# Four paired slabs in a row in gate and up, with a fifth weight place and the residual outside

## The chip, the cores and the metric

The kernel runs on one core of one Trainium2 chip. The metric is the device time in microseconds (us) of one execution; the time of the kernel before is the median of three runs.

## The reference, cut to what matters

One encoder layer over 256 rows of width 2048, everything in float32: four mixers side by side (gated linear attention, a Fourier mixer, a long convolution, a short convolution) whose outputs are joined and projected, a cross attention to 256 memory rows, a gated feed-forward part with a hidden width of 5632, and a last norm. The change lies in the feed-forward part:

```python
def swiglu(h, w_gate_up, w_down):
    gate, up = jnp.split(h @ w_gate_up, 2, axis=-1)
    return (jax.nn.silu(gate) * up) @ w_down
...
        x = x + mix @ w_out[l]
        x = x + cross_attention(rms_norm(x, norm_g[l, 1]), mem_n, w_xq[l], w_xkv[l], w_xo[l])
        x = x + swiglu(rms_norm(x, norm_g[l, 2]), w_gate_up[l], w_down[l])
    return rms_norm(x, final_norm_g)
```

## The kernel before

**Precision.** TensorE multiplies in a shortened 32-bit form, so each operand is split into a high part (a cast on ScalarE) and a low part (the rest, a subtraction on VectorE). One product of a 128x128 piece of features with a 128x512 piece of weights is three matmuls: high x high, high x low, low x high (`part`, L430 to L435).

**The weight stream.** All weights come as slabs of 128x2048 (1 MB) in the order in which they are used; class `Stream` loads each into one of three raw buffers (SP's queue), casts and subtracts it half by half into a *weight place*, and hands the halves to TensorE. There are three places in the pool `wp`, and a fourth in another pool while `extra` is set; `_fill` (L166) prepares up to three halves beyond the one in use. A half takes its place when TensorE is done with the one that had it.

**Plain and paired slabs.** In gate and up and in down the two row halves of the features and two column blocks of the weights form a 2x2 block product. A *plain* slab (N) holds 16 blocks and needs eight products. A *paired* slab (S) holds two feature blocks for two column blocks each, and does them with seven products (a Winograd scheme): the weights are also added up to sums, which makes four halves of 1024, 512, 1024 and 1024 columns (`_sums`, L140) instead of two of 1024, and the features are added up once into tiles `z` (`combine`, L437). In gate and up the first sum comes from memory ready made: in `_load` the last 512 columns are copied twice into a tile `two` and 1024 columns are accumulated onto it by a DMA from POOL's queue (L99 to L103), so VectorE adds twice per paired slab (L158); in down it adds four times.

**The stages around the change.** Gate and up takes its first 512 + 512 columns with eight plain slabs (L1125), then ten groups of eight slabs each (L1133), with the plan `GROUP`: paired slabs are the third, fifth and seventh. `mixed` (four 512-wide operations on VectorE) follows the last paired slab of a group, `gated` (two) the point at which the gate columns are done as well, `upped` (two additions, two scalings, two transposes, then two stores from POOL's queue to the memory tensor `hidden`) the end of the group. Down then runs over 44 blocks of 128 hidden features in two passes of 22 slabs; `PASSES[0]` begins with four plain slabs. Its first six pairs take slots 0 to 11, so its first plain slab uses slots 12, 13, 14 and 15 (`steps`, L471).

**What sets the order.** Instructions are put on their engines in written order where they can run, and a scheduler moves them up where their data and buffers allow. `keep_place` (L308) ties an instruction to the one written before it on its engine. Small work is written between the products by generators in class `Background` (L204). It keeps a debt of VectorE: `dve(n, ops)` adds n / 960 + 0.155 per operation, each product takes off 0.68 (`pe`, L226), and `poll`, called behind each product, steps a generator only where its time has come and the debt is under `OWED`, 0.9:

```python
    def poll(self):
        for e in list(self.q):
            if self.owed < OWED and self.now >= e[1]:
                self.step(e)
```

One generator is `fetch` (L1087): for block k it loads the turned tile of `hidden` into one of eleven `tmp` buffers (POOL's queue) and, some blocks later and not before 15 us behind the store, splits it into slot k of `f` (a cast on ScalarE and a 256-wide subtraction on VectorE, both tied by `keep_place`). `early` brings slots 0 to 21 while gate and up still runs; behind the last group `drain(early)` (L1135) writes whatever is left of it at once, and a second `fetch` brings the rest, which `ready` (L1188) forces block by block, three ahead of use.

**Memory.** `res` is the residual, four tiles of 128x1024 that gate and up does not touch. Slots of `f` are `act[4:12]`, fourteen tiles of their own, the three `z` tiles in halves, and the normed features `h3`.

Of the kernel before, what the change touches and what calls it, by code (L numbers as in the profile page):

```python
# [13 lines left out]
F32 = mybir.dt.float32  # L14
# [9 lines left out]
P = 128  # L24
# [20 lines left out]
GROUP = "NNSNSNSN"  # L45
# [3 lines left out]

PAIRED = {a + i for a, plan in [(GATE_UP + 8 * j, GROUP) for j in range(10)] + [(DOWN, PASSES[0]), (DOWN + 22, PASSES[1])]  # L50
          for i, x in enumerate(plan) if x == "S"}
SUMMED = {i for i in PAIRED if i < DOWN}

# [18 lines left out]
class Stream:  # L72


    def __init__(self, tc, pools, W, bg):
# [8 lines left out]
        self.extra = self.sums = None  # L84
# [3 lines left out]
    def _buffers(self, n, m):  # L88

        pool = self.extra if self.extra and len(self.halves) % 4 == 3 else self.wp  # L90
        at = 48 if any(a <= n < b for a, b in ROWS) else 8
        return (pool.tile([P, 1088], F32R, name=t, tag=t)[:, at:at + m] for t in ("wh", "wl"))

    def _load(self, n):
# [3 lines left out]
        if n // 16 + 1 in SUMMED:  # L98
            W, t = self.W[n // 16 + 1], self.sums.tile([P, 1024], F32, name="two", tag="two")  # L99
# [66 lines left out]
    def _fill(self):  # L166

        ahead = self.at + 1 + min(3 if self.extra else 2, self.n // 16)
        while len(self.halves) < ahead and self.made < NBLK:
            self._half()  # L170

# [82 lines left out]
class Block:  # L254
# [208 lines left out]
    def paired_rows(self, w, cols, slots, sums, plan, mixed, first, ready=None, late=0, before=None, swap=False):  # L463
# [12 lines left out]
        def put(name, hi, lo, wh, wl):  # L476
# [5 lines left out]
            left[name] -= 1  # L482
            self.part(q[name][:, :], hi, lo, wh, wl, new, left[name] == 0)

        form = lambda t, r: (t[:, r * P:(r + 1) * P], t[:, R + r * P:R + (r + 1) * P])
        n = done = 0
        for i, kind in enumerate(plan):
            if before:
                before(i)
            if kind == "S":  # L490
# [76 lines left out]
    def run(self):  # L567
# [21 lines left out]
        self.gk = [nc.dram_tensor(f"state{i}", (R, P), F32, kind="Internal").ap() for i in range(4)]  # L589
        self.vd = nc.dram_tensor("values", (P, 8 * 512), F32, kind="Internal").ap()  # L590
# [18 lines left out]
        with self.tc.tile_pool(name="wx", bufs=1) as st.extra:  # L609
# [257 lines left out]
    def attention(self, ps):  # L867
        tc, nc, act, st = self.tc, self.nc, self.act, self.st
        with tc.tile_pool(name="atp", bufs=1) as atp, tc.tile_pool(name="kp", bufs=1) as kp, \
# [111 lines left out]
            st.extra = None  # L981
# [47 lines left out]
    def mlp(self):  # L1029
        tc, nc, act = self.tc, self.nc, self.act  # L1030
        with tc.tile_pool(name="fp", bufs=1) as fp:
            self.gap(fp, 192)
            f = [fp.tile([P, 512], F32R, name=f"f{i}") for i in range(14)]
            z = [fp.tile([P, 1024], F32R, name=f"z{i}") for i in range(3)]
            f = act[4:12] + f + [z[i // 2][:, i % 2 * 512:i % 2 * 512 + 512] for i in range(6)] + self.h3
            with tc.tile_pool(name="wy", bufs=1) as self.st.extra:
                self.gap(self.st.extra, 64)
                with tc.tile_pool(name="tw", bufs=2) as self.st.sums, tc.tile_pool(name="gp", bufs=1) as gp:
# [8 lines left out]
    def gate_up(self, gp, f, z):  # L1047
# [74 lines left out]

        sums = [((2 * i, 2 * i + 1), z[i]) for i in range(GROUP.count("S"))]
        comb = self.bg.add(combined())
# [766 lines left out]
```

## Time and profile before

| what | us |
|---|---|
| median of 3 runs (lowest, highest) | 1436.53 (1435.76, 1437.61) |
| the profiled execution's own time | 1434.72 |
| its span | 1432.9 |
| TensorE busy | 1423.0 (99%) |
| VectorE busy | 1145.7 (80%) |
| ScalarE busy | 815.8 (57%) |

The span is the stretch that the profile covers; the profiled execution's own time is 1.82 us longer, and the median of the runs 1.81 us longer than that. Engines in the profile: PE is TensorE's matmuls, PEld its weight loads, DVE VectorE, ACT ScalarE, POOL GpSimd, SP the engine whose queue issues most loads. A timeline row has start, length, engine, source line, operation, out<-in and count, and in brackets the idle time before it with what ended it. Matmuls overlap, so their spacing counts, not their length.

### The profile page before, as it was taken

The page shows a single profiled execution, that of the slowest core. Times are in us where ns is not written, and L with a number is a line of the kernel's source. Part 1 is how long each engine was busy: PE and PEld are TensorE (multiplying, and loading weights), DVE is VectorE, ACT ScalarE, POOL GpSimd, SP SyncE. Part 2 cuts the span into 40 slices and gives each one's busy share as a digit, 9 for nine tenths or more (in the row PEclk, how much of TensorE's full clock was granted, in tenths as well). Part 3 has the DMA queues.
Part 4 walks back from the last instruction along what each step waited for, and adds up shares of the span by engine and source line. Part 5 has one row for each costly group of instructions (what it writes and reads, how often), then busy time and mean ns, then how long its engine had stood idle before and what let it go on. Part 6 is the DMA issues. An engine that isn't in the chain of part 4 may idle for free.

```text
span 1432.9 us, 18653 instructions
## 1 busy us (share of the span) xinstructions
PE 1423.0 (99%) x6589; PEld 1181.4 (82%) x6589; DVE 1145.7 (80%) x1738; ACT 815.8 (57%) x1183; POOL 234.6 (16%) x306
## 2 busy tenths in 40 slices
PE   9999999999999999999999999999999999999997
PEld 8888888888888888888888888888888888788886
DVE  6667868777877767777677888889888888989997
ACT  7556565446745555556455556555555556655655
POOL 0000100013212223531430121122011002000000
PEclk9999999999999999999999999999999999999999
DMA  9877554456667787865986989899999887665554
GB/s 350 299 291 247 205 202 166 171 172 224 198 199 232 235 271 246 275 201 171 287 242 207 283 280 289 275 275 285 294 293 289 264 265 227 217 231 180 193 219 147
DMA packets 73038, 343.80 MB, mean 240 GB/s; under 512 B 10957, under 2 KB 12654, under 8 KB 45168
## 3 DMA queue, kind: packets, MB, share of 16 engines
q1 hardware_dynamic: 54848, 288.98, 57.6%
q0 software_dynamic: 17664, 52.97, 15.6%
q8 instruction: 51, 0.84, 0.2%
q10 hardware_dynamic: 432, 0.66, 0.1%
q14 instruction: 43, 0.35, 0.1%
HBM read 322.12 MB, written 20.45 MB: 239 GB/s over the span
## 4 chain that ended last, share of the span: by engine, by line
PE 98%; DVE 1%; DMA 0%; ACT 0%; issue 0%; SPq 0%; ACTq 0%
PE pg L432 22%; PE pg L433 22%; PE pg L434 22%; PE pm L432 7%; PE pm L434 7%; PE pm L433 7%; PE pg L380 4%; PE pg L381 2%; PE pm L1344 1%; PE pm L1022 1%; PE pm L993 1%; PE pm L1753 0%; DMA raw<-in_W 0%; DVE res L282 0%; PE pm L994 0%; PE pm L1518 0%
## 5 line engine op out<-in xcount | busy, mean ns | idle before, releaser
L136 DVE TENSOR_TENSOR wl<-raw,wh 128x1024 fp32r<-128x1024 f32 (+1 forms) x413 | 494.1, 1211 | 167.6 <-ACT wh L135 164.8
L135 ACT CAST wh<-raw 128x1024 fp32r<-128x1024 f32 (+1 forms) x413 | 424.7, 1043 | 282.9 <-PE pg L434 188.3
L432 PE MATMUL pg<-wh,act 128*128 128x512 f32 (+1 forms) x1191 | 465.5, 391 | 0.0
L433 PE MATMUL pg<-wl,act 128*128 128x512 f32 (+1 forms) x1191 | 463.9, 389 | 0.1
L434 PE MATMUL pg<-wh,act 128*128 128x512 f32 (+1 forms) x1191 | 463.8, 390 | 0.0
L432 PEld LDWEIGHTS pg<-wh,act 128*128 128x128 f32 x1191 | 224.0, 188 | 47.9 <-issue 1.5
L434 PEld LDWEIGHTS pg<-wh,act 128*128 128x128 f32 x1191 | 223.9, 188 | 47.5 <-DVE act L282 0.6
L433 PEld LDWEIGHTS pg<-wl,act 128*128 128x128 f32 x1191 | 224.0, 188 | 46.5 <-DVE wl L136 1.2
L147 ACT CAST wh<-raw 128x1024 fp32r<-128x1024 f32 (+1 forms) x150 | 137.4, 921 | 149.6 <-PE pg L434 53.8
L148 DVE TENSOR_TENSOR wl<-raw,wh 128x1024 fp32r<-128x1024 f32 (+1 forms) x150 | 155.9, 1060 | 52.8 <-ACT wh L147 52.6
L433 PE MATMUL pm<-wl,act 128*128 128x512 f32 x309 | 120.3, 389 | 0.1
L432 PE MATMUL pm<-wh,act 128*128 128x512 f32 x309 | 120.2, 389 | 0.0
L434 PE MATMUL pm<-wh,act 128*128 128x512 f32 x309 | 120.2, 389 | 0.0
L380 PE MATMUL pg<-act,wh 128*128 128x512 f32 x256 | 90.5, 395 | 0.0
L381 PE MATMUL pg<-act,wl 128*128 128x256 f32 x256 | 71.8, 280 | 0.0
L433 PEld LDWEIGHTS pm<-wl,act 128*128 128x128 f32 x309 | 58.0, 188 | 12.3 <-DVE wl L136 0.4
L434 PEld LDWEIGHTS pm<-wh,act 128*128 128x128 f32 x309 | 58.0, 188 | 12.1
L432 PEld LDWEIGHTS pm<-wh,act 128*128 128x128 f32 x309 | 58.0, 188 | 12.0
L102 POOL DMA_DIRECT2D two<-in_W x30 | 26.6, 885 | 237.6 <-DMA two<-in_W 106.4
L158 DVE TENSOR_TENSOR raw<-raw 128x512 f32<-128x512 f32 x90 | 61.8, 687 | 1.2
L147 ACT CAST wh<-two 128x1024 fp32r<-128x1024 f32 x30 | 31.5, 1051 | 52.0 <-PE pg L434 27.0
L380 PEld LDWEIGHTS pg<-act,wh 128*128 128x128 f32 x256 | 48.1, 188 | 10.5
(375 smaller groups left out, 1819.3 us busy)
## 6 DMA issues: line engine op xcount, KB each, us to landing
raw<-in_W SPq DMA_DIRECT2D x216, 1024.0 KB, 5.6
raw<-in_W SPq DMA_DIRECT2D x30, 768.0 KB, 6.3
two<-in_W SPq DMA_DIRECT2D x60, 256.0 KB, 4.8
two<-in_W POOLq DMA_DIRECT2D x30, 512.0 KB, 9.0
raw<-in_W SPq DMA_DIRECT2D x11, 512.0 KB, 7.1
hidden<-g POOLq DMA_DIRECT2D x22, 256.0 KB, 3.8
tmp<-hidden POOLq DMA_DIRECT2D x44, 128.0 KB, 6.0
features<-tmp POOLq DMA_DIRECT2D x32, 128.0 KB, 5.2
```

Of the source, the lines that this page charges most:

```text
L102: nc.gpsimd.dma_start(t, W[:, 512:1536], accum_op=ALU.add)
L135: nc.scalar.copy(wh[:, a:b], r[:, a:b])
L136: nc.vector.tensor_tensor(out=wl[:, a:b], in0=r[:, a:b], in1=wh[:, a:b].bitcast(F32), op=ALU.subtract)
L147: nc.scalar.copy(wh, src)
L148: nc.vector.tensor_tensor(out=wl, in0=src, in1=wh.bitcast(F32), op=ALU.subtract)
L158: nc.vector.tensor_tensor(out=out, in0=a, in1=b, op=ALU.add)
L380: self.nc.tensor.matmul(p[:, :], wh, slot[:, :], start=start, stop=False)
L381: self.nc.tensor.matmul(p[:, 0:R], wl, slot[:, 0:R], start=False, stop=stop)
L432: self.nc.tensor.matmul(p, hi, wh, start=start, stop=False)
L433: self.nc.tensor.matmul(p, hi, wl, start=False, stop=False)
L434: self.nc.tensor.matmul(p, lo, wh, start=False, stop=stop)
L993: nc.tensor.matmul(p[:, :], q[d][:, r * P:(r + 1) * P], kt[d][:, :], start=d == 0, stop=False)
```

## The change

The plan of a group becomes two plain slabs, four paired in a row, two plain (`GROUPS`). The residual is stored to memory during gate and up's first slabs, its four tiles take the ready made sums in turn (`st.sums`), and it is loaded back behind the tenth group. `AHEAD` says with which earlier slab each ready made sum is loaded (slab 2 of a group with slab 6 of the group before, 3 with 0, 4 with 1, 5 with 3). The two `two` tiles go, and a fifth weight place `wz` comes in their room; places now form a list `ring`, the one used longest ago first, to which pools are lent and given back. There are four `z` tiles and twelve own `f` tiles, so `early` brings slots 0 to 19 and the second `fetch` 20 to 43. In gate and up each product is tied by `keep_place`. The code also knows a kind "s" (paired, without a ready made sum), which the plan does not use.

```diff
-GROUP = "NNSNSNSN"
+GROUPS = "NNSSSSNN",
...
+AHEAD = {2: -2, 3: 0, 4: 1, 5: 3},
+SUMS = {GATE_UP + 8 * j + a: GATE_UP + 8 * j + i for j in range(10) for i, a in AHEAD[j % len(GROUPS)].items()}
...
     def _buffers(self, n, m):
-        pool = self.extra if self.extra and len(self.halves) % 4 == 3 else self.wp
+        slot = min(self.ring, key=lambda x: x[1])
+        assert slot[1] < self.at or slot[1] < 0
+        pool, slot[1] = slot[0], len(self.halves)
...
-        if n // 16 + 1 in SUMMED:
-            W, t = self.W[n // 16 + 1], self.sums.tile([P, 1024], F32, name="two", tag="two")
+        if n // 16 in SUMS:
+            W, t = self.W[SUMS[n // 16]], self.sums[0]
+            self.sums.append(self.sums.pop(0))
...
-        ahead = self.at + 1 + min(3 if self.extra else 2, self.n // 16)
+        ahead = self.at + 1 + min(len(self.ring) - 1, self.n // 16)
...
+            mark = self.mark()
             self.part(q[name][:, :], hi, lo, wh, wl, new, left[name] == 0)
+            if w == "w_gate_up":
+                self.keep_place(mark)
...
-            f = [fp.tile([P, 512], F32R, name=f"f{i}") for i in range(14)]
-            z = [fp.tile([P, 1024], F32R, name=f"z{i}") for i in range(3)]
+            f = [fp.tile([P, 512], F32R, name=f"f{i}") for i in range(12)]
+            z = [fp.tile([P, 1024], F32R, name=f"z{i}") for i in range(4)]
...
-        sums = [((2 * i, 2 * i + 1), z[i]) for i in range(GROUP.count("S"))]
+        sums = [((2 * i, 2 * i + 1), z[(i + 1) % 4]) for i in range(4)]
...
+        def before(n):
+            if n == 1:
+                self.st.lend(self.wz)
+                for c, x in enumerate(whole):
+                    nc.sync.dma_start(self.rd[:, c * 1024:(c + 1) * 1024], x)
+                self.st.sums = list(whole)
+            if n in (1, 3):
+                self.bg.drain(self.late if n == 1 else last)
...
-        early = self.bg.add(fetch(0, FT - 22, 3, 2.0, 15))
+        early = self.bg.add(fetch(0, FT - 24, 3, 2.0, 15))
         self.bg.drain(comb)
         for j in range(1, DFF // 512):
-            upped(j, self.paired_rows("w_gate_up", [j * 512, DFF + j * 512], self.h3, sums, GROUP, mixed, gated, swap=j % 2 == 0)[0])
+            plan = GROUPS[(j - 1) % len(GROUPS)]
+            upped(j, self.paired_rows("w_gate_up", [j * 512, DFF + j * 512], self.h3, sums[:8 - plan.count("N")], plan, mixed, gated,
+                                      before=lambda i: (j, i) == (10, 5) and self.st.back(self.wz), swap=j % 2 == 0)[0])
+        for c, x in enumerate(whole):
+            nc.sync.dma_start(x, self.rd[:, c * 1024:(c + 1) * 1024])
         self.bg.drain(early)
-        self.fetch = self.bg.add(fetch(FT - 22, FT, 6, SOON))
+        self.fetch = self.bg.add(fetch(FT - 24, FT, 6, SOON))
```

More of the change, by code (lines that the diff above doesn't have):

```diff
@@ L83, in __init__ @@
         self.raw = None
-        self.extra = self.sums = None
+        self.ring = [[self.wp, -1] for _ in range(3)]
+        self.sums = []
         self.places = []
@@ L166, in _fill, with lend, back @@
     def _fill(self):
-        ahead = self.at + 1 + min(3 if self.extra else 2, self.n // 16)
+        ahead = self.at + 1 + min(len(self.ring) - 1, self.n // 16)
         while len(self.halves) < ahead and self.made < NBLK:
             self._half()
+    def lend(self, pool):
+        self.ring.append([pool, -1])
+        return pool
+    def back(self, pool):
+        self.ring = [x for x in self.ring if x[0] is not pool]
     def _used(self):
@@ L608, in run @@
         nc.scalar.copy(self.identr, self.ident)
[L609 removed]
+        with self.tc.tile_pool(name="wx", bufs=1) as self.wx:
+            st.lend(self.wx)
             self.attention(self.mixers())
```

25 lines of the change are left out of this document (14 added, 11 removed).

## The prediction

> **What bounds the kernel now.** I read the page first (engine shares, chain), then the windows table cut at the ten groups, then timelines of one group and of the passage from gate and up to down.
>
> ```profile
> PE 1423.0 (99%) x6589; PEld 1181.4 (82%) x6589; DVE 1145.7 (80%) x1738; ACT 815.8 (57%) x1183; POOL 234.6 (16%) x306
> ...
> PE 98%; DVE 1%; DMA 0%; ACT 0%; issue 0%; SPq 0%; ACTq 0%
> ```
>
> The chain is TensorE for 98% of the span, so a matmul taken away shortens the kernel unless another wait fills its place. The windows table: gate and up's first slabs, two of the ten groups, the passage, the first part of down:
>
> ```profile
> core 0: us, PE busy (x) PEld busy (x) DVE busy (x) ACT busy (x) POOL busy (x), PEclk, DMA share, GB/s
> 690.00:775.00 85.00, 85.00 (x377) 70.24 (x375) 61.11 (x108) 48.16 (x73) 26.11 (x33) 1.00 0.82 254
> ...
> 982.00:1023.50 41.50, 41.50 (x185) 34.37 (x184) 36.88 (x47) 24.49 (x30) 7.06 (x9) 1.00 0.92 275
> ...
> 1106.50:1148.00 41.50, 41.50 (x185) 34.38 (x184) 35.20 (x41) 23.26 (x25) 3.83 (x5) 1.00 0.90 268
> ...
> 1189.50:1231.00 41.50, 41.47 (x184) 34.01 (x183) 38.93 (x62) 24.18 (x39) 12.98 (x15) 1.00 0.82 254
> 1231.00:1317.00 86.00, 85.96 (x378) 70.38 (x377) 79.47 (x133) 50.49 (x74) 0.00 (x0) 1.00 0.53 196
> ```
>
> TensorE has no gap in a group, VectorE is busy 85 to 89% of it, and the DMA engines 90 to 92%. So the gain is certain to be asked for, and two engines stand close behind. One product (three matmuls) takes 0.68 us, from the starts of two successive L432 in TensorE's timeline:
>
> ```profile
> 982.00 0.39 PE L432 MATMUL pg<-wh,act 128*128 128x512 f32 x1
> ...
> 982.68 0.39 PE L432 MATMUL pg<-wh,act 128*128 128x512 f32 x1
> ```
>
> **Term 1, the fourth paired slab.** A plain slab is eight products, a paired one seven. A group goes from 5 x 8 + 3 x 7 = 61 products (41.5 us, as the row) to 60 (40.8). Ten groups: 10 x 0.68 = 6.8 us less on the path.
>
> **Term 2, four paired slabs in a row against VectorE.** VectorE's timeline over one paired slab:
>
> ```profile
> 1001.33 1.82 DVE L148 TENSOR_TENSOR wl<-raw,wh 128x1024 fp32r<-128x1024 f32 x2
> 1003.07 0.68 DVE L158 TENSOR_TENSOR raw<-two,raw 128x512 f32<-128x512 f32 x1
> 1003.78 0.69 DVE L158 TENSOR_TENSOR raw<-raw 128x512 f32<-128x512 f32 x1
> 1004.39 0.41 DVE L282 TENSOR_TENSOR f<-tmp,f 128x256 fp32r<-128x256 f32 x1
> 1005.05 1.23 DVE L148 TENSOR_TENSOR wl<-two,wh 128x1024 fp32r<-128x1024 f32 x1 [0.24 <-ACT wh L147]
> ...
> 1019.45 3.50 DVE L136 TENSOR_TENSOR wl<-raw,wh 128x1024 fp32r<-128x1024 f32 x3 [0.21 <-ACT wh L135]
> ```
>
> Three subtractions in 3.50 us with a last one of 1.22 start 1.14 apart. The first two of the slab take 1.74 to the next start (1.14 + 0.60), the two additions 0.71 + 0.61. A paired slab is 3 x 1.14 + 0.60 + 1.32 = 5.34 us of VectorE against 7 x 0.68 = 4.76 of TensorE; a plain one 2.28 against 5.44. Per group VectorE grows by 5.34 - 2.28 = 3.1 us, to about 38.3 of 40.8: it fits on average, but inside the run it falls behind by 0.58 us a slab. What covers it is the fifth place, four halves ready while one is in use. The refill, from ScalarE's timeline beside TensorE's:
>
> ```profile
> 987.90 0.39 PE L434 MATMUL pm<-wh,act 128*128 128x512 f32 x1
> ...
> 988.37 1.05 ACT L147 CAST wh<-raw 128x1024 fp32r<-128x1024 f32 x1 [0.29 <-PE pm L434]
> ```
>
> The last matmul of a half would be followed at 988.13, the cast starts 0.25 later and takes 1.05, the subtraction follows. Let the run start at 0: its first four halves are ready, half 5 is split by 0.25 + 1.05 + 1.2 = 2.5, and VectorE then works without rest: 4.4 after half 6 and its additions, 6.7 after half 8, then 5.34 a slab. The tightest half is the third of the last slab, ready at 6.7 + 5.34 + 1.14 + 0.60 + 1.32 + 1.14 = 16.2; TensorE asks for it at 3 x 4.76 + 3 x 0.68 = 16.3. It holds by 0.1 us. With four places it would not (each refill starts a half later). Every 0.1 us more per slab costs 0.3 a group, 3 us in all. Bounds: 0 and 6 us (0.2 a slab off). I take 0.5, near the end the rows give.
>
> **Term 3, the planner's debt and what it holds back.** This is the term that decides. The background generator `fetch` brings the gated products back and splits them into the slots that down needs; it steps only where the planner's debt is under 0.9. The debt is counted from the code: a 1024-wide half 1.22, a 512-wide operation 0.69, two 512 additions 1.38, a 256-wide split 0.42; each product takes off 0.68. Before, a group adds 10 x 1.22 + 3 x 5.73 for the halves and 8.26 for `mixed`, `gated` and `upped`: 37.7 against 61 x 0.68 = 41.5, so it returns to nothing in each group and four splits a group go through. By that count the 22nd is written in the sixth group's slab 5. The trace agrees (these are the casts of the 22 splits):
>
> ```profile
> L290 ACT CAST act<-tmp x8: 397/401/404, 794.3 to 880.5; 128x256 fp32r<-128x256 f32 x8
> ...
> L290 ACT CAST f<-tmp x14: 398/400/402, 885.6 to 1013.6; 128x256 fp32r<-128x256 f32 x14
> ```
>
> After, a group adds 8 x 1.22 + 4 x 5.73 + 8.26 = 40.95 against 60 x 0.68 = 40.80. The debt never runs off: each group ends 0.15 higher, 0.42 more for each split. Counted half by half (halves written four ahead) its lowest points, at the end of a group's second slab, are 0 in the first group (loads only, the split must wait 15 us), 0.29 in the second (one split), 0.87 in the third (one split), then 1.44 and 0.15 more each time, to 2.4 in the tenth. So two of the 20 early splits go through, and 18 wait for `drain(early)` behind the tenth group. `keep_place` ties each to the VectorE instruction written before it, the last transpose of `upped`, so none can be pulled forward. Down's first plain slab starts with slots 12, 13, 14, 15. Before, all were there long before down's first product:
>
> ```profile
> L432 PE MATMUL pg<-wh,f x46: 389/389/393, 1192.8 to 1297.2; 128*128 128x512 f32 x46
> ...
> 1194.64 1.27 DVE L282 TENSOR_TENSOR h<-h,pm 128x512 f32<-128x512 f32 x2
> 1195.84 1.40 DVE L286 SCALAR_TENSOR_TENSOR h<-h,rc,g 128x512 f32<-128x512 f32 x2
> 1197.16 1.29 DVE L557 STREAM_TRANSPOSE g<-h 128x512 f32<-128x512 f32 x2
> 1198.38 3.45 DVE L136 TENSOR_TENSOR wl<-raw,wh 128x1024 fp32r<-128x1024 f32 x3
> ...
> 1203.43 0.76 DVE L282 TENSOR_TENSOR z<-tmp,z 128x256 fp32r<-128x256 f32 x2
> ...
> 1222.13 0.75 DVE L282 TENSOR_TENSOR act<-tmp,act 128x256 fp32r<-128x256 f32 x2
> ```
>
> `upped` takes 1198.38 - 1194.64 = 3.7 us on VectorE after the group's last product; splits follow one another by 0.75 - 0.41 = 0.34. The loads are not tied, and POOL's timeline shows loads of down's late slots issued over 100 us before their splits (the first of those stands at 1203.43 above), as far as the eleven `tmp` buffers go:
>
> ```profile
> 1038.81 3.53 POOL L564 DMA_DIRECT2D tmp<-hidden  x4 [4.59 <-issue]
> ...
> 1081.49 2.65 POOL L564 DMA_DIRECT2D tmp<-hidden  x3 [5.58 <-issue]
> ...
> 1198.15 1.52 POOL L559 DMA_DIRECT2D hidden<-g  x2 [30.44 <-DVE g L557]
> 1205.09 6.18 POOL L564 DMA_DIRECT2D tmp<-hidden  x7 [5.41 <-DVE tmp L282]
> ...
> tmp<-hidden POOLq DMA_DIRECT2D x44, 128.0 KB, 6.0
> ```
>
> So loads 2 to 12 are in their buffers, eleven of them, and load 13 waits for the first split. From the last product at 0: `upped` ends at 3.8, splits 2 to 12 at 3.8 + 11 x 0.34 = 7.5, product of slot 12 from 7.6 (1.36 us of work). POOL stores the hidden tiles first (to about 5.2), load 13 then takes 6.0 and its cast and subtraction 0.8: 12.0. Slots 14 on follow 0.88 apart (6.18 / 7), faster than the 1.36 that TensorE needs. Idle: 7.6, and 12.0 - 7.6 - 1.36 = 3.0: 10.6 us. If load 13 had a buffer too it is 8; if only nine of the eleven are held by these loads, 13. I take 10. What no longer stands there, `mixed` and `gated`, is done two slabs earlier, so VectorE isn't fuller behind the stall; I put nothing for it, at most 3 us for a first paired slab of down whose sums come late.
>
> **Term 4, the clock after the stall.** At the very start TensorE's 256-wide matmuls stand 0.21 us apart, then 0.12:
>
> ```profile
> 1.07 4.64 PE L601 MATMUL pm<-ones 128*128 128x128 f32 x20 [1.07 <-DVE eps L602]
> ...
> 5.72 0.41 PE L433 MATMUL pg<-wl,act 128*128 128x256 f32 x1
> 5.93 0.41 PE L434 MATMUL pg<-wh,act 128*128 128x256 f32 x1
> ...
> 7.11 0.28 PE L434 MATMUL pg<-wh,act 128*128 128x256 f32 x1
> 7.23 0.28 PE L432 MATMUL pg<-wh,act 128*128 128x256 f32 x1
> ```
>
> Half speed lasted up to 6.8, 5.7 us from the first matmul. Before has no idle stretch that shows whether a stall brings it back. If it does, the loss is at most half of 5.7, 2.9 us; if not, nothing. Part of it would lie under the wait for load 13. I take 1. The Trainium skill, "TensorE: Matmul & The Clock Gate", Part 1, says that an idle window of about 3.4 us halves the clock and that some 3.4 us of work release it. By that rule the loss would be about 1.7 us, and it speaks against the change; the starting rows fit it, and no run here yet shows a stall of that length.
>
> **The edits at nothing.** The residual's store (2 MB, four SP issues in gate and up's first slabs) and its return lie in stages with room, 0.82 and 0.53 of the DMA engines by the windows rows, and three raw buffers stand between SP and TensorE. Uncovered, each would be 2.1 MB at the 275 GB/s of the row, 7.6 us. On SP the return stands ahead of raw loads two slabs before use. The fourth `combine` is beside plain slabs. The written order costs nothing: the rows shown run in it already.
>
> **The DMA engines.** One group (the window from 934.87 to 976.36) has these shares by queue (packets, MB, share); the last line is the page's rate by slice:
>
> ```profile
> q1 hardware_dynamic: 2018, 9.18, 63.7%
> q0 software_dynamic: 801, 2.69, 29.7%
> ...
> GB/s 350 299 291 247 205 202 166 171 172 224 198 199 232 235 271 246 275 201 171 287 242 207 283 280 289 275 275 285 294 293 289 264 265 227 217 231 180 193 219 147
> ```
>
> 9.18 MB in 63.7% of 41.5 is 347 GB/s; q0 takes 12.3 us for 2.69 MB. A paired for a plain slab adds 0.26 MB to q1 (0.75 us) and one 0.52 MB accumulation to q0 (2.4 us at q0's rate): 38.8 + 3.2 = 42 us against 40.8, less the loads that no longer pass. The excess is 1.2 us a group at the end where rates stay, nothing where a fuller queue is faster. Loads run two slabs (10 us) ahead, so I put 0.
>
> **Sum.** -6.8 + 0.5 + 10 + 1 = +4.7 us. On the profiled execution, 1434.72 (span 1432.9), that is 1439.4; the median of the runs, 1436.53, is 1.8 above it, so I give 1441.2 for the median.
>
> **The rivals.** A, the splits do pass: something (a debt lower than my count by 0.6 where it is lowest) lets four a group through. Then term 3 and 4 go. For it: eight lowest points are under 2.4, not far from 0.9. Against it: the same count places the 22 splits of before. Price: -6.8, plus a split or two inside the paired run, which has 0.1 us to spare (0.7 us in five groups): -6.8 + 3.5 to -6.8, about 1431.5. B, VectorE loses the run: its order there isn't the written one, or an addition waits; from 0.3 us a slab on, each group loses 0.9, 9 us in ten: -6.8 + 9 + 11 = +13 with term 3, +2 without. For it: a margin of 0.1 us. Against it: before, VectorE idles 4.6 to 6.3 us of each group (the rows above), part of it for lack of a place, and a fifth is added. C, the DMA engines bound the groups: 1.2 us each, +12 on top of -6.8, about +5 without term 3 and +16 with it. For it the 42 against 40.8, against it that fuller queues ran faster: 350 GB/s in the page's first slice. D, the change does less than it says: a product order that already holds can't change time; it decides nothing.
>
> **How the numbers follow.** Term 3 as counted: 0.62. A: 0.23. B: 0.10. C: 0.05. No change is what lies within 0.2% (2.9 us), about what a measurement of this kernel can tell. The likeliest case runs from +1 (8 of stall, no clock loss) to +10, so a quarter of it, 0.16, falls within 0.2%, and 0.02 below for what I may have missed; 0.44 is slower, with B and C 0.59. A gives 0.22 faster and 0.01 the same: 0.24, 0.17, 0.59 in all. Alone the likeliest case has 1437.5 to 1446.5; with A below and B above the range is 1430.5 to 1447.
>
> **What would show it.** Right: group period 40.8 us; TensorE idle some 10 us in one or two pieces behind the tenth group, released by a split on VectorE; the casts of `fetch` absent between the third group and the end; one burst of eighteen. Wrong: casts of `fetch` spread over the groups and no gap there (A); gaps at the fourth paired slab's third half in every group (B); casts waiting for raw with TensorE behind them (C).

## The result and the profile after

The changed kernel takes 1494.6 us (median of 4 runs, 1491.7 to 1496.6) against 1436.1 (median of 4, 1435.4 to 1437.6): a ratio of 1.040, interval 1.0385 to 1.0424. The forecast was 1441.2 with a range up to 1447. Slower was the likeliest side, but the loss, 58.5 us, is twelve times the 4.7 forecast. The profiled execution took 1496.58 us, its span is 1494.5 (before: 1432.9), so 61.6 us have to be found.

Shares and chain of the changed kernel, from its page:

```profile
PE 1440.3 (96%) x6559; PEld 1176.8 (79%) x6559; DVE 1177.0 (79%) x1786; ACT 826.7 (55%) x1205; POOL 243.0 (16%) x316
...
PE 26%; DVE 10%; DMA 7%; issue 7%; ACT 3%; POOL 0%; SPq 0%; ACTq 0%; DVEq 0%; POOLq 0%
```

TensorE is no longer the whole chain (98% before); VectorE and the DMA engines have come into it. The windows table, cut at the same three stages in both kernels, first after, then before:

```profile
690.00:780.00 90.00, 85.41 (x367) 69.78 (x366) 62.08 (x116) 47.89 (x74) 29.26 (x36) 0.96 0.93 291
780.00:1235.00 455.00, 426.47 (x1802) 336.74 (x1801) 377.96 (x438) 238.63 (x271) 57.81 (x68) 0.99 0.87 264
1235.00:1320.00 85.00, 73.81 (x312) 58.60 (x311) 73.94 (x135) 49.09 (x89) 29.58 (x34) 0.96 0.82 227
```

```profile
690.00:780.00 90.00, 90.00 (x399) 74.38 (x398) 64.61 (x113) 50.26 (x75) 26.15 (x34) 1.00 0.81 251
780.00:1195.00 415.00, 415.00 (x1832) 343.71 (x1831) 357.02 (x420) 235.08 (x272) 67.76 (x79) 1.00 0.90 278
1195.00:1280.00 85.00, 84.93 (x373) 69.17 (x372) 79.95 (x141) 50.89 (x82) 12.98 (x15) 1.00 0.63 212
```

Second number is TensorE's busy time. Before it fills all three stages; after it has holes in all three. I added up every start-to-start distance of TensorE's matmuls beyond 0.227 us (its steady distance): 7.3 us are lost in gate and up's first stage, 47.0 in the ten groups, 14.7 in the passage and down's first part. With the 6.8 that the fourth paired slab saves, that is +62.2 against the 61.6 measured (the kernel before loses 1.1 in the same three). The period of a group (distance of the casts of the product q1, first to last of the ten) is 45.8 us; before it was 41.5, and 40.8 was forecast.

The three places, in rows. **The passage**, TensorE's timeline, with ScalarE's casts for down's slots and POOL's loads for them:

```profile
1240.40 0.39 PE L449 MATMUL pm<-wh,act 128*128 128x512 f32 x1
1249.84 0.79 PE L447 MATMUL pg<-wh,f 128*128 128x512 f32 x1 [9.05 <-ACT f L305]
1250.43 0.63 PE L448 MATMUL pg<-wl,f 128*128 128x512 f32 x1
1250.86 0.63 PE L449 MATMUL pg<-wh,f 128*128 128x512 f32 x1
...
1252.57 0.50 PE L447 MATMUL pg<-wh,f 128*128 128x512 f32 x1
1252.91 0.40 PE L448 MATMUL pg<-wl,f 128*128 128x512 f32 x1
1253.14 0.39 PE L449 MATMUL pg<-wh,f 128*128 128x512 f32 x1
```

```profile
1241.25 1.32 ACT L305 CAST f<-tmp 128x256 fp32r<-128x256 f32 x4
...
1249.39 0.40 ACT L305 CAST f<-tmp 128x256 fp32r<-128x256 f32 x1 [5.87 <-DMA tmp<-hidden]
...
1245.38 11.52 POOL L582 DMA_DIRECT2D tmp<-hidden  x13
```

One stall, ended by a split of down's slot (line 305, `fetch`), then matmuls 0.43 apart until 1252.6. The split itself waited for its load, the first of the thirteen that POOL issues from 1245.38 on. **The first stage**, ScalarE's timeline beside TensorE's:

```profile
736.88 2.94 ACT L143 CAST wh<-raw 128x1024 fp32r<-128x1024 f32 x3 [8.97 <-DMA raw<-in_W]
```

```profile
734.60 0.39 PE L449 MATMUL pg<-wh,act 128*128 128x512 f32 x1
738.92 0.80 PE L447 MATMUL pg<-wh,act 128*128 128x512 f32 x1 [3.94 <-ACT wh L143]
740.37 0.80 PE L448 MATMUL pg<-wl,act 128*128 128x512 f32 x1 [0.65 <-DVE wl L144]
740.97 0.63 PE L449 MATMUL pg<-wh,act 128*128 128x512 f32 x1
```

ScalarE waited 9.0 us for a raw load; TensorE stood still for 3.9 us, and for 0.65 more until the subtraction behind the cast was done. **The groups**, the table of waits over nine of the ten groups (total, times, longest), and VectorE's and TensorE's timelines inside one run of four:

```profile
ACT wh L143 <- DMA raw<-in_W: 81.1, 25, 7.3
ACT wh L155 <- DVE raw L166: 54.9, 19, 5.7
...
PE pg L448 <- DVE wl L156: 10.9, 15, 1.5
PE pm L448 <- DVE wl L156: 10.3, 14, 1.5
```

```profile
942.02 0.69 DVE L166 TENSOR_TENSOR raw<-res,raw 128x512 f32<-128x512 f32 x1
942.62 1.22 DVE L156 TENSOR_TENSOR wl<-res,wh 128x1024 fp32r<-128x1024 f32 x1
943.76 0.68 DVE L166 TENSOR_TENSOR raw<-raw 128x512 f32<-128x512 f32 x1
945.01 1.23 DVE L156 TENSOR_TENSOR wl<-res,wh 128x1024 fp32r<-128x1024 f32 x1 [0.57 <-ACT wh L155]
946.16 1.22 DVE L156 TENSOR_TENSOR wl<-raw,wh 128x1024 fp32r<-128x1024 f32 x1
```

```profile
944.92 0.39 PE L449 MATMUL pg<-wh,z 128*128 128x512 f32 x1
945.97 0.49 PE L447 MATMUL pg<-wh,z 128*128 128x512 f32 x1 [0.67 <-ACT wh L155]
947.43 0.50 PE L448 MATMUL pg<-wl,z 128*128 128x512 f32 x1 [0.96 <-DVE wl L156]
```

Casts of plain slabs wait 81.1 us for raw in the groups; from 690 to 1330 it is 92.9, before over the same stretch 33.0. And in the rows the halves are out of order. The half split at 942.62 is the third slab's summed one, at 945.01 comes the fourth slab's summed half, and only at 946.16 the third slab's last half, for which TensorE has waited since 945.1 and goes on at 947.43. Where nothing ties them, the scheduler puts the instructions of one engine in an order of its own; a summed half hangs on nothing but its tile, so it overtakes the half that hangs on an addition, which then waits on ScalarE and VectorE. So there were two candidates for the groups, order and data, and the experiments had to part them.

### The profile page after: what moved, and what is told of

Same layout as the page of the kernel before. It is cut to its first block, busy times and chain, and to the rows that moved or that the text cites. A ratio compares the mean times of both kernels' runs of the same rounds, so it can differ in the third digit from the quotient of the medians.

```text
span 1494.5 us, 18686 instructions
## 1 busy us (share of the span) xinstructions
PE 1440.3 (96%) x6559; PEld 1176.8 (79%) x6559; DVE 1177.0 (79%) x1786; ACT 826.7 (55%) x1205; POOL 243.0 (16%) x316
## 4 chain that ended last, share of the span: by engine, by line
PE 26%; DVE 10%; DMA 7%; issue 7%; ACT 3%; POOL 0%; SPq 0%; ACTq 0%; DVEq 0%; POOLq 0%
DMA raw<-in_W 6%; PE pg L448 5%; PE pg L449 5%; DVE wl L156 5%; PE pg L447 5%; PE pm L448 4%; PE pm L449 3%; PE pm L447 3%; DVE raw L166 2%; ACT wh L155 2%; DVE wl L144 1%; ACT wh L143 1%; DMA ar<-features 1%; DVE h L297 0%; DVE h L301 0%
## 5 line engine op out<-in xcount | busy, mean ns | idle before, releaser
L447 PE MATMUL pg<-wh,act 128*128 128x512 f32 (+1 forms) x1166 | 458.2, 393 | 4.9 <-ACT wh L143 4.8
L448 PE MATMUL pg<-wl,act 128*128 128x512 f32 (+1 forms) x1166 | 456.5, 392 | 2.7 <-DVE wl L144 2.4
L449 PE MATMUL pg<-wh,act 128*128 128x512 f32 (+1 forms) x1166 | 456.1, 391 | 1.2 <-DVE act L297 1.2
L447 PEld LDWEIGHTS pg<-wh,act 128*128 128x128 f32 x1166 | 220.2, 189 | 53.2 <-ACT wh L143 6.0
L449 PEld LDWEIGHTS pg<-wh,act 128*128 128x128 f32 x1166 | 219.9, 189 | 48.3 <-DVE act L297 2.6
L448 PE MATMUL pm<-wl,act 128*128 128x512 f32 x284 | 111.4, 392 | 0.3 <-DVE wl L156 0.2
L447 PE MATMUL pm<-wh,act 128*128 128x512 f32 x284 | 111.2, 392 | 0.0
L449 PE MATMUL pm<-wh,act 128*128 128x512 f32 x284 | 111.0, 391 | 0.0
L110 POOL DMA_DIRECT2D res<-in_W x40 | 35.2, 881 | 239.0 <-DMA res<-in_W 113.9
L166 DVE TENSOR_TENSOR raw<-raw 128x512 f32<-128x512 f32 x100 | 68.5, 685 | 0.8
L449 PEld LDWEIGHTS pm<-wh,act 128*128 128x128 f32 x284 | 53.6, 189 | 11.1
L447 PEld LDWEIGHTS pm<-wh,act 128*128 128x128 f32 x284 | 53.5, 188 | 11.3
L448 PE MATMUL pm<-wl,z 128*128 128x512 f32 x112 | 45.8, 409 | 10.8 <-DVE wl L156 10.8
```

Of the source, the lines that this page charges most:

```text
L110: nc.gpsimd.dma_start(t, W[:, 512:1536], accum_op=ALU.add)
L166: nc.vector.tensor_tensor(out=out, in0=a, in1=b, op=ALU.add)
L447: self.nc.tensor.matmul(p, hi, wh, start=start, stop=False)
L448: self.nc.tensor.matmul(p, hi, wl, start=False, stop=False)
L449: self.nc.tensor.matmul(p, lo, wh, start=False, stop=stop)
```

## The experiments

Theories at the start: L, the loads come late (the sums' transfers crowd the raw loads); V, VectorE loses the run of four; P, the passage is the planner's debt, as forecast. Each diff is against the changed kernel. Where no interval is given the time is that of a single execution, beside 1435.8 to 1438.2 for the kernel before, run beside them; the changed kernel's own four runs spread over 4.9 us, so a difference of 5 us between two such times is little by itself, and the traces have to carry it. "Period" is the mean of nine group periods. Experiments 1, 2 and 6 leave out work that the result needs.

**1. No sum loads.**

```
-            for a in (0, 512):
-                nc.sync.dma_start(t[:, a:a + 512], W[:, 1536:2048])
-            nc.gpsimd.dma_start(t, W[:, 512:1536], accum_op=ALU.add)
```

> The changed kernel with the ready made sums never loaded: the two copies and the accumulation per paired slab of gate and up are left out, and whatever stands in the residual's tiles takes their place. VectorE's, ScalarE's and TensorE's work is the same. Theory L (loads: in each group the sum loads are issued while the paired run goes on and fill the DMA engines just before and under the plain slabs' raw loads, the casts of plain slabs come late, and the run starts with no halves in hand): a group falls from 45.8 us to 40.8 to 41.3, the casts' wait for raw in the groups from 81 us to under 10, and the first stage loses under 3 us instead of 7: 1440 to 1450. Theory V (VectorE's 5.34 us per paired slab against 4.76 doesn't fit whatever the loads do): groups stay at 45 and the time at 1485 to 1495. Theory P (the planner's debt) is not touched: some 9 us of idle TensorE behind the tenth group in either case.

1468.9 us, period 43.7 (41.9 to 46.2). The first stage's loss is gone (0.05 us), the passage's stall of 9.1 stays. So the sums' transfers make the whole of the first stage's loss. They don't make the whole of the groups': 2.9 us a group stay over 40.8, and what TensorE waits for longest there are subtractions on VectorE (12.2 us).

**2. No additions.** `ops` is left empty for summed slabs, the debt is still counted.

> The changed kernel with VectorE's two additions per paired slab of gate and up left out (1.3 us a slab); the planner's debt counts them still, and all loads stay. VectorE then needs 4.0 us per paired slab against TensorE's 4.76. L alone: the casts still wait some 60 to 80 us for raw, and TensorE loses less in the run only as far as VectorE can catch up, 41 to 42.5 us a group, 1447 to 1465. V alone: groups at 40.8, 1445 to 1450, and no rise of the casts' wait for raw beyond that of before (44 us in the groups). Stays at 45 a group: neither.

1471.0 us, period 43.1; casts wait 102.3 us for raw in the groups, more than in the changed kernel. VectorE's load went down by 5 us a group and the late data showed in its place. Neither theory holds alone.

**3. The splits let through**: at slabs 0, 1, 6 and 7 of each group the early `fetch` is stepped whatever the debt.

```
+            if i in (0, 1, 6, 7) and e:
+                self.bg.step(e[0])
```

> The changed kernel with the early generator stepped at the start of the slabs 0, 1, 6 and 7 of each group whatever the debt is, so that four splits go through a group. P: the 9.2 us gap behind the tenth group and the half speed after it (together some 11 us) go, no burst of eighteen casts stands there; the groups change by little, 0 to 1 us each in groups two to six: 1481 to 1490. If the gap has another cause (upped, the return of the residual, a weight place given back) it stays: 1492 to 1498.

1484.9 us, 9.7 less, and no stall behind the tenth group. P holds.

**4. Loads in order**: `keep_place` on SP's raw loads and sum copies from the group stage on. (POOL's accumulating transfers, where an expectation names them, are not held by this tie; they follow their copies by data.)

> The changed kernel with SP's copies for the sums and its raw loads tied to written order from two slabs before the groups to the end of gate and up, so that a sum's copies can't be issued slabs ahead of their place. The same bytes and the same work. L in its form 'early and bunched': the casts' wait for raw falls by half or more, groups 41 to 43.5, 1450 to 1475. L in its form 'too many bytes at any order': groups 44 to 46, 1480 to 1495. V: no change, 1490 to 1498.

1487.9 us: 0.15 us lost in the first stage, the groups unchanged at 45.6, so the numbers of the second reading. SP's timeline, first of the changed kernel, then of this one, shows why:

```profile
692.51 2.83 SPq L1152 DMA_DIRECT2D residual<-res  x2
696.14 3.53 SPq L116 DMA_DIRECT2D raw<-in_W  x2
699.72 2.15 SPq L109 DMA_DIRECT2D res<-in_W  x2
704.72 0.33 SPq L116 DMA_DIRECT2D raw<-in_W  x1
```

```profile
693.27 2.83 SPq L1162 DMA_DIRECT2D residual<-res  x2
696.90 14.35 SPq L123 DMA_DIRECT2D raw<-in_W  x4
```

The first group needs its sums at about 790. Their copies stand on SP at 699.7, among the raw loads, because the tile they go to was free and nothing held them back.

**5 to 8. Halves in order**, alone, without sum loads, with the loads' tie, and with the splits too. The tie is a mark ahead of each cast, subtraction and addition of the groups and `keep_place` behind it.

```
+        if GATE_UP <= n // 16 < DOWN:
+            mark = self.blk.mark()
+            self._write(n)
+            return self.blk.keep_place(mark)
```

> The changed kernel with the casts, subtractions and additions of gate and up's ten groups kept in the order in which they are written (one line ties each to the instruction written before it on its engine); nothing else differs. In the kernel without sum loads the groups with a period of 45 to 46 us have the summed half of the fourth paired slab split ahead of the last half of the third (929.92 ahead of 931.07), and a plain half ahead of the last paired one; the others, at 42.2, don't. Theory O (an order on VectorE and ScalarE that isn't the written one costs these groups 3 to 4 us): groups fall by about 2 us on average, about 1475 us, and no paired half is split ahead of an earlier one. Theory L (raw loads that land late by themselves): periods stay at 45 to 46, 1490 to 1496. Theory V (the run against VectorE even in the best order): 1490 or a little more, since an order that is fixed can only wait longer.

> The same tie, and the two copies and the accumulating transfer of each paired slab left out (the sums are then wrong, the work on all engines the same). Without the tie this was 1468.85 with periods of 41.9 to 46.2. Theory O: all groups at about 42, 1456 us. Theory V: VectorE's run still costs 1.4 us a group over 40.8, so 42.2 in every group and not less, 1456 to 1458; if the tie itself brings 40.8, V falls and the time is about 1445. Theory L (raw loads late even without sums): the periods of 44 to 46 stay, 1468.

> The tie on the halves together with the tie on the loads (SP's raw loads and sum copies and POOL's accumulations in written order), which alone gave 1487.94 with groups unchanged at 45.4 and the first stage's 7 us gone. Theory O: groups at 42 to 43, about 1462. Theory L in the form of too many bytes at any order (about 42 us of transfers a group): groups at 43 to 44, 1470 to 1475. If neither order matters to the groups: 1488.

> The same as the one before, and the early splits of down let through two a slab at slabs 0, 1, 6 and 7 of each group, which alone was worth 9.7 us (1484.89 against 1494.6). Expected 9 to 10 us under the kernel with both ties: 1452 by theory O, 1460 to 1465 by theory L. If groups at 40.8 were reached it would be about 1432; I expect that the loads forbid it.

| | sums loaded | no sum loads |
|---|---|---|
| order as the scheduler has it | 1494.6, period 45.8 | 1468.9, 43.7 |
| halves in order | 1489.6, 44.1 | 1449.2, 41.1 |
| halves and loads in order | 1465.6, 42.7 | |
| and splits let through | 1456.8, 43.5 | |

Alone, the halves' tie missed the 1475 that order was to bring. Its period fell by 1.7, but outside the nine periods, in the last slab of the tenth group, experiments 5, 6 and 7 lose 5.0 to 5.4 us that the changed kernel does not lose there (TensorE waits 2.5 us for a cast in experiment 6, then 0.8 for a subtraction, and the half clock follows). Why that half comes late stays open; the fifth place is given back and the residual's loads are issued shortly before. Experiments 7 and 8 lie between their two readings.

The second column is the verdict on V. Without sum loads and in order, the windows table over nine groups reads:

```profile
809.55:1179.53 369.98, 369.98 (x1625) 303.92 (x1624) 345.02 (x397) 215.03 (x245) 20.60 (x26) 1.00 0.59 200
```

TensorE has no hole that the busy time shows (2.0 us of small waits in all), 41.1 us a group, with the same additions and subtractions on VectorE (345 us, 93%). VectorE can keep up with four paired slabs in a row; order costs 19.7 us there. With both ties the sum loads add 16.4 (1449.2 to 1465.6), and casts then wait 40.4 us for raw loads (1.5 in experiment 6) and none for a summed tile. Order in all its parts is worth 29.0 where the sums are loaded, and neither tie alone shows it in the time (5.0 and 6.7).

What the DMA engines have to do is read from share times period over the nine groups. With both ties, and with the plan of experiment 15 further down:

```profile
811.09:1195.21 384.12, 375.16 (x1622) 301.81 (x1621) 345.23 (x397) 213.12 (x244) 51.70 (x61) 1.00 0.94 287
```

```profile
811.24:1186.92 375.68, 370.72 (x1620) 302.61 (x1619) 349.69 (x415) 220.05 (x263) 67.92 (x79) 1.00 0.98 298
```

0.94 x 384.12 / 9 = 40.1 us a group, 40.9 in the other; without sums 0.59 x 369.98 / 9 = 24.3. Four sums are 15.8, one is 4.0 us of all 16 engines. These are estimates from shares: a plain slab takes at most 3.5 us (24.3 for 7 MB of raw loads a group), a paired one 2.6 + 4.0 = 6.6 against TensorE's 4.76. Summed up by use, a run of four is 26.4 us of transfers in 19.0 us of products. But the loads are not issued by use: by `AHEAD` three of the four sums go with slabs 6, 0 and 1, so the densest stretch is the plain slabs 6, 7, 0 and 1, 4 x 3.5 + 3 x 4.0 = 26.0 us of transfers in 21.8 us of products, behind by 4.2; over the run itself, 14.4 in 19.0, they catch up.

**9. Groups of four and of three by turns**, with both ties (`GROUPS = "NNSSSSNN", "NNSNSNSN"`).

> Groups with four paired slabs in a row alternate with groups of three with a plain slab after each (the plan of the kernel before, its sums loaded one slab ahead), loads and halves in written order. The theory as it stands: a group of four costs 41.0 us when its halves are in order and its data has landed (measured without the sum loads), its transfers take about 40.3 us of the DMA engines (share times period in the kernel with both ties), so it runs at 42.7 because the loads fall behind; a group of three has 38 of 41.5 and lets them catch up. Then groups at 41.0 and 41.5, the splits of down pass in the groups of three and the 9 us behind the tenth group are gone: 1433 to 1437, level with before. If loads fall behind inside each group of four whatever its neighbours do: 42.7 in five groups, 1441 to 1445.

1446.6 us, ratio 1.0079 (1.0064 to 1.0093), period 42.5. No stall behind the tenth group, but the groups of four still lose beside neighbours that have room: the second reading.

**10. Three paired slabs a group**: all of the change but its fourth slab (`GROUPS = "NNSNSNSN",`).

> Everything of the change but the fourth paired slab: the residual outside, its tiles for the sums, five places, the products in written order, with the plan of the kernel before (three paired slabs apart, sums one slab ahead). Theory: what the groups lost came from the run of four, so groups stay at 41.5 and no gap stands behind the tenth; the residual's store in gate and up's first slabs is gone from the way of the loads, because sums are not asked for two slabs early there: 1436 to 1439; if the store alone makes the first stage's 7 us, 1443. Rival: the residual's tiles or the written order slow the groups by themselves, 1450 or more.

1453.2 us, ratio 1.0122 (1.0103 to 1.0140): the rival. 8.5 us are lost in the first stage, where SP has the sums' copies at 700.5 though the plan asks for them one slab ahead, and the period is 42.2.

**11. Products free**: without the `keep_place` on gate and up's products.

> The changed kernel without the line that keeps gate and up's products in written order. Theory: TensorE waits because data comes late, and the halves come in an order close to the written one, so another order of products saves little: 1488 to 1497. Rival T: the written order keeps TensorE waiting for a late half while products of halves that are ready could go first (the summed half of the next slab is split ahead of the last half of this one): 1480 or less.

1486.5 us, 8 less: between the two readings. The written order on TensorE costs something while halves come out of order, but it is no main cause.

**12. Two pairs, one slab's sums by VectorE** (`NNSSNSsN`, both ties, splits at slabs 0, 1, 4).

> Four paired slabs a group, in two pairs with a plain slab between and one behind (NNSSNSsN), the fourth with its sums made by VectorE from the whole slab and no sum loads; loads and halves in written order, the early splits let through two a slab at slabs 0, 1 and 4. It moves about 3.6 us of transfers a group away from the DMA engines (36.7 of 40.8 left) and adds 1.3 us of VectorE (39.6 of 40.8). Theory of the bytes: casts hardly wait for raw, groups at 41 to 41.5, no gap behind the tenth: 1432 to 1440. Rival V: VectorE has 1.2 us of room a group and the splits take 1.5, so it falls behind instead: groups at 42 to 43, 1445 to 1455.

1436.7 us, period 41.5, casts wait 7.0 us for raw in the groups. Level with the kernel before.

**13 to 15.** The VectorE slab first in its pair (`NNSSNsSN`, splits at slabs 0 and 1); experiment 10 with both ties; and two pairs with all sums by transfers (`NNSSNSSN`, otherwise as 12).

> The plan NNSSNsSN: as the last kernel, but the slab whose sums VectorE makes stands first in the second pair, behind the plain slab, and the early splits go through at slabs 0 and 1 alone. In the last kernel TensorE waited 0.9 to 1.2 us at the last half but one of that slab in the groups at 42, with a split inside the second pair and VectorE at 94 to 98%. Theory: the plain slab ahead gives VectorE 3.2 us of slack for the four additions, so the groups run at 41.0 to 41.2 and the time is 1431 to 1434, 2 to 5 us under the kernel before. Rival V: VectorE at 98% on average can't be ordered away; 41.5 a group as before, 1436 to 1438.

> The change without the fourth paired slab, as measured at 1453, now with loads and halves in written order. Theory O: what it lost (8.5 us in the first stage, 0.7 us a group) came of the order in which the loads and halves were put once the fifth place and the residual's tiles changed their dependencies: 1436 to 1440. Rival: the residual's 2 MB and the tiles cost it by themselves whatever the order: 1447 or more.

> NNSSNSSN with loads and halves in written order and the splits at slabs 0, 1 and 4, all sums by transfers. It differs from the kernel at 1436.74 only in who makes the fourth slab's sums, and from the one at 1456.79 in the plan's order. Theory of the bytes: some 40.3 us of transfers a group, groups at 42.5 to 43, 1448 to 1455. Rival (the length of the run matters and not the bytes): level with 1437.

13: 1441.1, ratio 1.0033 (1.0023 to 1.0043), a miss. 14: 1443.6, between its two readings; the tie takes the first stage's 8.5 us to 0.05, so there it was order and not the residual's bytes. 7.7 us stay in three groups (45.3, 42.9 and 44.0); in the first of these an accumulation stood on POOL behind loads of hidden tiles, before which POOL had rested 11.2 us, and TensorE waited 2.2 us for the half made from it. 15: 1438.9, period 41.7 at a DMA share of 0.98, with the same bytes as the kernel of experiment 8. My theory of the bytes (42.5 to 43) fell. By the order in which its loads are issued, two pairs never fall behind by more than 2.1 us (7.5 for a plain slab with a sum, in 5.4), where the run of four falls behind by 4.2, and casts wait 26.9 us for raw loads instead of 40.4. A run of two is also a shorter run for VectorE, and this experiment does not part the two. Its splits also stand at other slabs than in 8 (0, 1, 4 instead of 0, 1, 6, 7), so of the 17.9 us between the two a part may be theirs; against experiment 7, which forces no splits through, the period is 0.9 us shorter.

**16 and 17.** The plan of 12 with splits at slabs 0 and 1 and the residual's return spread over down's slabs 2 to 8; and the same with POOL's accumulations tied as well.

> The plan NNSSNSsN of the kernel that gave 1436.74 (raw loads, sum copies and halves in written order, one slab's sums by VectorE), with two edits: the early splits go through at slabs 0 and 1 alone, and the residual's return is issued in four pieces at slabs 2, 4, 6 and 8 of down, no longer beside the last raw loads of gate and up. In that kernel the groups without a split in the second pair had 41.0 to 41.1 and three groups 41.7 to 42.6 with a TensorE wait of 0.9 to 1.2 us on VectorE at their end. Theory (what is left are those two things): ten groups at 41.1, 1431 to 1434, under the kernel before by 2 to 5 us. Rival V (VectorE at 96 to 98% loses somewhere else): 1436 to 1440.

> The same, with POOL's accumulating transfers kept in written order as well (the ties so far hold raw loads and sum copies on SP only; the accumulations were free). In the kernel of three in order, an accumulation stood 11 us behind loads of hidden tiles on POOL and TensorE lost 2.2 us behind it. Theory (POOL's order matters where the splits pass): up to 2 us less than its twin. Rival: in written order an accumulation waits for its own copies with the hidden stores and loads behind it, and the splits wait: level or up to 3 us more.

16: 1442.2, ratio 1.0049 (1.0033 to 1.0066), over both of its readings. The later groups ran at 41.1 to 41.5 as expected, but the first four at 42.0 to 42.4, with a wait of TensorE for VectorE of 1.0 to 1.2 us at each one's end; VectorE is busy 96% over the nine groups. 17: 1447.6, ratio 1.0075 (1.0062 to 1.0088), 5.4 over its twin: the way of the rival, by more than it allowed. That an accumulation then waits with the hidden tiles behind it is the rival's reason; it is argued and not read from rows. No version beat the kernel before; the best, 12, is level by a single execution.

## Why the prediction was wrong, and where it was right

**Term 1** held: 60 products, 41.1 us a group in experiment 6, with 0.2 to 0.3 of small waits.

**Term 3**, the step that was said to decide, was right in its mechanism: the debt holds the splits back, and they stand in a burst behind the tenth group. Stall forecast 10 (8 to 13), measured 9.2, one gap, released by a split; letting the splits through gave 9.7 back. That the size came so near is in part luck. Two early splits were counted and one went through (its cast stands at 843.0), so eleven buffers reached slot 11 and not 12. The forecast had 7.6 us for the burst and 3.0 more for slot 13's load; the rows have a single wait for slot 12's load, which was issued at 1245.38 and let its cast start at 1249.39, 4.0 us where 6.0 was taken. What comes late after it, put at nothing and bounded by 3, cost 2.9 more than before in down's first part.

**Term 4** was right in kind and size: after the stall the matmuls stand 0.43 apart for 2.7 us (1249.84 to 1252.57 in the rows above), which loses 1.5. Forecast 1. The granted clock of that stretch is 0.50. By the rule of the Trainium skill, "TensorE: Matmul & The Clock Gate", Part 1, the estimate was 1.7; the trace agrees that a stall of 9 us halves the clock, and shows 2.7 us of work where that page has some 3.4 until it is released.

**Term 2** is the step that failed, 0.5 forecast. Its walk is nearly right: in written order and with data in time a group with a run of four takes 41.1, where 40.85 was forecast. But it took the written order of the halves for the order that runs, and gave no reason. The changed kernel ties only the products; casts, subtractions and additions are free. The prediction's one word on order, "the rows shown run in it already", is on the products, and was read from groups in which every paired slab has a plain slab behind it. With a run of four the fourth slab's summed half overtakes the third slab's last one. In place of 0.05 us a group, that order costs 2.5 (43.65 against 41.11, experiments 1 and 6). Rival B named this ("its order there isn't the written one") at 0.10 and priced it at 0.9.

**The DMA engines**, put at 0, were the other half. The count, 42 us a group, was near (40.1 to 40.9 measured) and its average does fit; but the sentence "Loads run two slabs ahead (10 us), so I put 0" compares averages. Rival C had it at 1.2 us a group; with both ties it is 1.6 (42.7 against 41.1), and casts wait for raw loads. That the densest stretch makes this, 4.2 us behind in the run of four against 2.1 in two pairs, fits experiments 7, 9 and 15 (40.1 us of transfers a group lose more in 7 than 40.9 in 15), but is not shown alone: the shorter run on VectorE and the order on POOL's queue changed or stayed free with it.

B and C are not rivals but add up: 2.5 us a group for order alone, 1.6 for the loads alone, 4.7 for both (45.8 against 41.1), so 0.6 of it comes from their meeting. Together they make most of the 47 us in the groups, where the two prices, added, were some 21; what was most under-priced is order, at 0.9 for 2.5.

**The side.** Slower, at 0.59, came true in the main by luck: terms 3 and 4, the reasons given for it, make 10.7 us, and the groups, put at 0.5, make 47.

**The edits at nothing.** The residual's store was priced by its bytes, at most 7.6. The first stage did lose 7.3, but for another reason: the residual's tiles come free early, and what was to be loaded into them two slabs ahead of use was issued 90 us ahead. Experiments 1, 4 and 14 each take that away while the store stays. The products' written order, put at nothing, cost 8 us beside the halves out of order (experiment 11, a single execution). The fifth place and the return were not tried alone.

Open: why the plans with two pairs miss the 1431 to 1434 that 41.1 a group would give, by 3 us (a single execution of 12) to 8 (16). In 12, 6.2 of the 6.6 us that TensorE loses in the groups stand at the slab whose sums VectorE makes. VectorE at 96% with the splits is what the rows show; it was not parted from POOL's queue.

## What to carry to other kernels

An edit that frees a buffer or lengthens a run also frees the scheduler: before a margin of tenths is walked through, find out which instructions are tied to their written order, and on which queues. A stage that fits by its average share of the DMA engines can still lose to late loads (1.6 us a group here); compare transfers with products stretch by stretch, in the order in which the loads are issued, before putting it at nothing. Where there are two causes, a single repair can show little in the time: each tie alone gave back 5 to 7 us here, both 29. A table of both causes, each taken away alone and together, shows what each is worth.

## What the runs showed of the hardware

Two short stalls close together also bring the half clock back, where they fall into the same stretch of some 3.4 us. TensorE's timeline in experiment 1:

```profile
929.77 0.39 PE L446 MATMUL pg<-wh,z 128*128 128x512 f32 x1
930.89 0.50 PE L444 MATMUL pg<-wh,z 128*128 128x512 f32 x1 [0.73 <-ACT wh L152]
932.34 0.50 PE L445 MATMUL pg<-wl,z 128*128 128x512 f32 x1 [0.95 <-DVE wl L153]
...
933.51 0.63 PE L446 MATMUL pm<-wh,act 128*128 128x512 f32 x1
```

Idle stretches of 0.73 and 0.95 us, and from 933.1 to 936.5 the matmuls stand 0.43 apart. In the changed kernel 0.67 and 0.96 us at 945.97 and 947.43 (rows above) did not do it: the next matmuls are 0.23 apart. The granted clock tells the two apart. In every run its changes lie on a grid with a step of 3.413 us: in experiment 1 at 933.16, 936.58, 1195.99, 1199.40, 1216.47 and 1226.71. From 929.75 to 933.16, one step of this grid, TensorE is idle for 1.68 us, and the next step has clock 0.50; in the changed kernel the two stretches fall into two steps, the fuller one (945.58 to 948.99) with 1.36 us idle, and the clock stays. Over all runs, from 700 to 1400 us, no step at full clock with less than 1.59 us of idle is followed by half clock, all 22 with more than 1.94 are, and of the 14 between these 9. The Trainium skill, "TensorE: Matmul & The Clock Gate", Part 1, asks for an idle window of about 3.4 us, though it also tells of a kernel whose short idle stretches made the clock oscillate. The grid of the runs agrees with that length; but in experiment 1 no single idle stretch was that long, and the clock fell all the same, so here the measurement decides.

A summed tile, two copies of 256 KB and an accumulating transfer of 512 KB, took 4.0 us of all 16 engines by the shares above, as much as 1.15 MB of raw loads, for its 1 MB.
